# A second scan that draws dense work behind two of its three steps, with a bias moved into a gate, divided transposes and other PSUM banks

## The chip, the cores and the metric

The kernel runs on one core of a Trainium2 chip. Its time is the device time of one execution in microseconds (us); 1247.04 us is the median of three runs. The engines are PE (matrix products), DVE (element-wise work, 32x32 transposes), ACT (activations, copies), POOL, and SP, which issues DMAs. Each takes its instructions strictly in the order in which the program puts them on its queue, and waits where an operand or a buffer is not ready. PE writes into PSUM only; its banks are given out here by four tags, "mm", "aux", "e" and "us", with two tiles of 128x512 each.

## The reference, cut to what matters

The model has two residual layers, each with a token mixer and a gated FFN with a causal convolution. The mixer of the second is RWKV-7: projections, a state that is updated token by token, a norm per head, a bonus and a gate.

```python
def wkv7_scan(r, w, k, v, a, b):
    def step(state, inp):
        r_t, w_t, k_t, v_t, a_t, b_t = inp
        sa = jnp.einsum('bhvk,bhk->bhv', state, a_t)
        state = (state * w_t[:, :, None, :]
                 + sa[..., None] * b_t[:, :, None, :]
                 + v_t[..., None] * k_t[:, :, None, :])
        y_t = jnp.einsum('bhvk,bhk->bhv', state, r_t)
        return state, y_t
...
    y = wkv7_scan(r_h, decay, k_h, v_h, -kk, kk * a_h)
    mean = jnp.mean(y, -1, keepdims=True)
    var = jnp.mean(jnp.square(y - mean), -1, keepdims=True)
    y = ((y - mean) * lax.rsqrt(var + GN_EPS)).reshape(B, S, D)
    y = y * ln_w.astype(f32) + ln_b.astype(f32)
    bonus = jnp.sum(r_h * k_h * r_k.astype(f32), -1, keepdims=True) * v_h
    y = (y + bonus.reshape(B, S, D)).astype(h.dtype)
    return (y * g) @ w_o
```

There are 512 positions, 1024 channels, 16 heads of 64.

## The kernel before, in words

Activations lie transposed, as 8 tiles of 128 channels by 512 positions. Every dense product is made with a high and a low part of both operands, three matmuls of 128x512 (L325, L326, L327) for each 128 channels of the sum; we call these **dense work**. A dense product over 8 tiles of channels is thus 24 matmuls into one bank.

The mixer works on chunks of 64 positions, 8 chunks, and on two groups of 8 heads (4 tiles) each. For each group it first makes the operands and products of all chunks (`pairs`, L973 and L988, with DVE's masks at L977), inverts a triangular 64x64 matrix for each chunk and head (`invert`), and then scans over the chunks (`scan`).

*Inversion.* DVE transposes 32x32 blocks (`turn`, L1051: ix to li), eliminates column by column in pairs of operations (L1069, L1070), and transposes the result twice (ix<-li, the block inverses, and li<-li, the same once more turned). PE joins the blocks: L1090 needs ix, L1093 what came of L1090 and the second transposes, and copies on ACT lie between (L1098, L1103, L1105). Group 0 turned its 32 column blocks with one instruction, group 1 with four of 8. The inversion of group 0 ends before the first scan, that of group 1 runs beside the first scan.

*Value and bonus.* For each tile m, `projections` makes a dense product, copies it to `v` (L854), and `value` transposes it with a centring matrix (L868) and copies it out. When the pair's products are there, L883 sums the bonus per head, L885 multiplies it by v into `rt`, and L886 adds `ln_b` on ACT. The result waits in `rt` for the norm (L1366) and for the gate (L1209).

*Scan.* One chunk has five batches of small matmuls in three steps. Step 1: L1301 (us), from which `wt` is copied (L1304), and L1305. Step 2: the solve L1314, from which `vu` is copied, one half by DVE (L1315) and one by ACT (L1316). Step 3: L1321, from which the next chunk's `vu` is summed (L1325, two instructions), and L1326, from which `y` is copied (L1329). Behind each second chunk `finish` norms two chunks' y (L1342 square, L1347, L1357), transposes it (L1363) and adds it into `rt` (L1366).

*The order.* `weave` (L1467) runs the scan as `main` and draws dense work from `fill`, a chain of generators: value projections, gate products (L1135, the gates themselves L1201 to L1214), then the output product. At each `yield` of the scan a debt grows by `rate`; for each whole unit one step of `fill` (two tiles of channels, 6 matmuls, or a piece of a gate) is emitted, to be placed behind the PE instruction that ended the step `lag` steps earlier. For the second scan the rate is 0.72 and the lag 2. When the gates wait for the norm of group 0, a step of `fill` is two matmuls without use (`idle`, L1124). What the scans have not drawn comes behind them. A scheduler then settles each queue's order.

Of the kernel before, what the change touches and what calls it, by code (L numbers as in the profile page):

```python
# [12 lines left out]
F32 = mybir.dt.float32  # L13
# [7 lines left out]
P = 128  # L21
D = 1024
KT = 8
# [121 lines left out]
class Emit:  # L145
# [622 lines left out]
    def rwkv_main(self, r, ctx, gain):  # L768
# [39 lines left out]
        def projections():  # L808
# [29 lines left out]
            for m in range(KT):  # L838
                a = self.acc("mm")
                w = load.take()  # L840
                if m == KT - 2:
                    ga["w"] = load_gate(0)
                for n, _ in enumerate(self.dense_steps(a, w, xv)):
                    yield
                    next(late, None)
                    if m == KT - 1 and n == 0:
                        gw[0] = gate_weights(ga["w"])
                        ga["parts"] = self.gate_parts()
                    if m == KT - 1 and len(gx) < 2:
                        gx.append(gate_mix(len(gx)))  # L850
                for _ in late:
                    yield
                v = ip.tile([P, T], F32, tag="v", bufs=1, name=self.uid("v"))
                S.copy(v, a)  # L854
                late = value(m, v)
# [3 lines left out]
        def value(m, v):  # L859
# [21 lines left out]
            S.activation(wb, self.c("bones", P), AF.Copy, scale=self.p("r_k", m))  # L881
            q = bank()
            nc.tensor.matmul(q, wb, rt[g][:, i, :], start=True, stop=True)  # L883
            b = rt[g][:, i, :]
            V.tensor_tensor(b, q, v, ALU.mult)  # L885
            S.activation(b, b, AF.Identity, bias=self.p("ln_b", m))  # L886
            vdone.add(m)
# [139 lines left out]
        def invert(g):  # L1027
# [21 lines left out]
            def turn(out, src):  # L1049
                for bs in [slice(n, n + 8) for n in range(0, 32, 8)] if g == 1 else [slice(0, 32)]:  # L1050
                    V.transpose(out[:, bs], src[:, bs])  # L1051
# [151 lines left out]
        def gate(g, i, ts, q=None):  # L1203

            if q is None:
                q = self.acc("aux")[:, 0:ts.stop - ts.start]
                opening(g, i, ts, q)
            o = rt[g][:, i, ts]
            V.tensor_tensor(o, o, q, ALU.mult)  # L1209
            while len(outs[g]) <= i:  # L1210
                outs[g].append(tuple(self.xr.tile([P, T], F32R, tag=t, bufs=10, name=self.uid(t)) for t in ("mxh", "mxl")))
            oh, ol = (x[:, ts] for x in outs[g][i])
            S.copy(oh, o)
            V.tensor_tensor(ol, o, oh.bitcast(F32), ALU.subtract)  # L1214
# [52 lines left out]
        def scan(g, late=iter(())):  # L1267

            ih = [(i, hd) for i in range(4) for hd in (1, 0)]
            y = None  # L1270

# [11 lines left out]
            for c in range(NCH):  # L1283
# [19 lines left out]
                wt = tile_([P, 4, C], "wt", 4)  # L1303
                V.tensor_copy(wt, us[:, 0])  # L1304
                batch(lambda i, hd, n: nc.tensor.matmul(e[H[hd], 0, i, :], st[i][H[hd], 0:C], vu[H[hd], hd, i, :],  # L1305
# [5 lines left out]
                self.step(late)  # L1311
                yield
                for i, hd in ih:
# [3 lines left out]
                self.step(late)  # L1317
                yield
                lead = None
# [10 lines left out]
                self.step(late)  # L1330
                yield
                if c % 2 == 1:
# [134 lines left out]
    def weave(self, main, side, fill, rate, lag, side_rate=0.5, ktiles=2):  # L1467
# [5 lines left out]
        n0 = len(nc.cur_bb.bb.instructions)  # L1473
        for _ in main:
            new = nc.cur_bb.bb.instructions[n0:]
            pe = [i for i in new if i.engine == mybir.EngineType.PE]
            marks.extend(pe[-1:] or marks[-1:])
            due += rate
            side_due += side_rate if side else 0
# [3 lines left out]
            while due >= 1:  # L1483
                due -= 1
                if len(marks) > lag:
                    with tc.issue_after(marks[-1 - lag]):
                        next(fill, None)
# [37 lines left out]
```

## Time and profile before

| | us |
|---|---|
| median of three runs | 1247.04 |
| the runs | 1244.97, 1247.04, 1248.28 |
| profiled execution | 1245.55 |
| its span, first to last instruction | 1243.7 |
| start of the first scan's L1301, of the second scan's | 725.8, 784.2 |
| start of the second scan's last L1326 | 839.6 |
| mean granted PE clock over the span | 0.996 |

Times in the rows are in us from the span's start, durations in us or, with "mean ns", in ns. A row of the order of time has the start, the duration, the engine, the line, the operation, what it writes and reads, and in brackets how long the engine had been idle and what ended that. Matmuls are pipelined: 128x512 shows as 0.39 although the next one starts 0.23 later, so costs of PE are read from start to start. A row of a stretch has its limits and length, the busy time of PE, of PE's weight loads, of DVE, ACT and POOL, the granted PE clock, the DMA engines' share and GB/s.

### The profile page before, as it was taken

The numbers are of one execution on the slowest core, as the hardware profiler recorded it, in microseconds if no ns is written. First come the engines' busy times: TensorE is split into PE (matmuls) and PEld (weight loads), VectorE is DVE, ScalarE is ACT, GpSimd is POOL, SyncE is SP. The second block draws the span as 40 slices with busy tenths as digits, with TensorE's granted clock in tenths as the row PEclk, the third lists the DMA queues.
The fourth block names the chain that finished last, engine by engine and source line by source line (L and its number), as shares of the span: only waits on it lengthen the run. The fifth ranks groups of instructions, "written<-read, shape, count | busy, mean of one in ns | idle before, by whom it ended". The sixth has DMA issues, their size and how long they took to land.

```text
span 1243.7 us, 19411 instructions
## 1 busy us (share of the span) xinstructions
PE 1226.8 (99%) x7535; PEld 1000.2 (80%) x7535; DVE 851.1 (68%) x1418; ACT 633.1 (51%) x1089; POOL 81.4 (7%) x106
## 2 busy tenths in 40 slices
PE   9999999999999999999999999999999999999997
PEld 6878888888888888877887777778888888888886
DVE  5566578888876454675899698776777777872323
ACT  6544455555554343466787667424544444543232
POOL 1100200000000001000000013222000000000000
PEclk9999999999999999999999899999999999999999
DMA  7232457887556776326888797654223223333332
GB/s 273 94 105 82 132 180 246 246 249 241 192 172 193 220 226 196 109 81 182 220 242 237 188 280 233 219 171 135 85 102 102 90 97 102 97 88 104 97 93 81
DMA packets 125133, 201.65 MB, mean 162 GB/s; under 512 B 39857, under 2 KB 63153, under 8 KB 125041
## 3 DMA queue, kind: packets, MB, share of 16 engines
q10 hardware_dynamic: 38976, 112.87, 29.5%
q1 hardware_dynamic: 86064, 87.54, 22.6%
q8 instruction: 59, 0.97, 0.3%
q14 instruction: 34, 0.27, 0.1%
HBM read 152.93 MB, written 47.45 MB: 161 GB/s over the span
## 4 chain that ended last, share of the span: by engine, by line
PE 91%; DVE 4%; DMA 3%; ACT 1%; issue 0%; SPq 0%; POOL 0%; DVEq 0%; POOLq 0%; ACTq 0%
PE mm L325 9%; PE mm L327 9%; PE mm L326 9%; PE aux L325 6%; PE aux L326 6%; PE aux L327 6%; PE e L325 6%; PE e L326 6%; PE us L325 6%; PE e L327 6%; PE us L327 6%; PE us L326 6%; PE us L1314 1%; PE aux L973 1%; PE aux L988 1%; PE us L1321 1%
## 5 line engine op out<-in xcount | busy, mean ns | idle before, releaser
L237 ACT CAST w<-w 128x512 fp32r<-128x512 f32 x340 | 206.5, 611 | 359.8 <-PE aux L327 92.6
L238 DVE TENSOR_TENSOR w<-w,w 128x512 fp32r<-128x512 f32 x340 | 230.5, 680 | 180.2 <-ACT w L237 179.6
L325 PE MATMUL mm<-mxh,w 128*128 128x512 f32 x408 | 167.9, 412 | 2.7 <-DVE rt L885 2.6
L327 PE MATMUL mm<-mxh,w 128*128 128x512 f32 x408 | 161.1, 395 | 0.0
L326 PE MATMUL mm<-mxl,w 128*128 128x512 f32 x408 | 160.6, 394 | 0.0
L325 PEld LDWEIGHTS mm<-mxh,w 128*128 128x128 f32 x408 | 77.0, 189 | 22.8 <-DVE rt L885 3.3
L327 PEld LDWEIGHTS mm<-mxh,w 128*128 128x128 f32 x408 | 77.0, 189 | 17.1 <-issue 0.8
L326 PEld LDWEIGHTS mm<-mxl,w 128*128 128x128 f32 x408 | 77.1, 189 | 16.2 <-issue 1.7
L575 ACT ACTIVATE cv<-z,par 128x512 f32<-128x512 f32 x88 | 71.7, 817 | 26.5 <-DVE z L573 21.2
L325 PE MATMUL aux<-mxh,w 128*128 128x512 f32 x216 | 84.5, 391 | 0.0
L325 PE MATMUL us<-mxh,w 128*128 128x512 f32 x216 | 84.5, 391 | 0.0
L327 PE MATMUL aux<-mxh,w 128*128 128x512 f32 x216 | 84.2, 390 | 0.0
L326 PE MATMUL aux<-mxl,w 128*128 128x512 f32 x216 | 84.1, 389 | 0.0
L326 PE MATMUL us<-mxl,w 128*128 128x512 f32 x216 | 84.1, 389 | 0.0
L327 PE MATMUL us<-mxh,w 128*128 128x512 f32 x216 | 84.1, 389 | 0.0
L354 POOL TENSOR_TENSOR ss<-ss,sq 128x512 f32<-128x512 f32 x24 | 31.7, 1323 | 761.1 <-ACT sq L352 761.1
L325 PE MATMUL e<-mxh,w 128*128 128x512 f32 x208 | 81.4, 391 | 0.0
L326 PE MATMUL e<-mxl,w 128*128 128x512 f32 x208 | 81.1, 390 | 0.0
L327 PE MATMUL e<-mxh,w 128*128 128x512 f32 x208 | 81.0, 389 | 0.0
L576 DVE SCALAR_TENSOR_TENSOR cv<-z,par,cv 128x512 f32<-128x512 f32 x88 | 66.0, 752 | 19.5 <-ACT cv L575 19.5
L577 DVE SCALAR_TENSOR_TENSOR cv<-z,par,cv 128x512 f32<-128x512 f32 x88 | 66.0, 752 | 2.9
L325 PEld LDWEIGHTS aux<-mxh,w 128*128 128x128 f32 x216 | 40.5, 188 | 9.0 <-issue 0.5
(1113 smaller groups left out, 2555.2 us busy)
## 6 DMA issues: line engine op xcount, KB each, us to landing
w<-in_wup ACTq DMA_DIRECT2D x88, 512.0 KB, 3.7
w<-in_wdn ACTq DMA_DIRECT2D x32, 512.0 KB, 3.7
st<-std SPq DMA_DIRECT2D x15, 640.0 KB, 6.6
w<-wkd ACTq DMA_DIRECT2D x16, 512.0 KB, 5.1
w<-wvd ACTq DMA_DIRECT2D x16, 512.0 KB, 5.1
w<-wod ACTq DMA_DIRECT2D x16, 512.0 KB, 4.2
w<-in_wdn ACTq DMA_DIRECT2D x16, 384.0 KB, 3.3
w<-in_wsu ACTq DMA_DIRECT2D x8, 512.0 KB, 3.7
```

What stands on the lines that cost most here:

```text
L237: nc.scalar.copy(hi[r, :n], src)
L238: (lo_eng or nc.vector).tensor_tensor(lo[r, :n], src, hi[r, :n].bitcast(F32), ALU.subtract)
L325: mm(acc, wh, xh, start=first, stop=False)
L326: mm(acc, wh, xl, start=False, stop=False)
L327: mm(acc, wl, xh, start=False, stop=last)
L354: nc.gpsimd.tensor_tensor(self.ss, self.ss, self.sq, ALU.add)
L575: nc.scalar.activation(c, z[:, 2:], AF.Identity, scale=cw(2, i), bias=self.p("conv_b", l * 44 + i))
L576: nc.vector.scalar_tensor_tensor(c, z[:, 1:T + 1], cw(1, i), c, ALU.mult, ALU.add)
L577: nc.vector.scalar_tensor_tensor(c, z[:, 0:T], cw(0, i), c, ALU.mult, ALU.add)
L973: nc.tensor.matmul(qs[hd][:, c - ch.start, :], bk[H[hd], c, C * hd:C * hd + P], ar[H[hd], c, :], start=True, stop=True)
L988: nc.tensor.matmul(qs[hd][:, c, :], bk[H[hd], c, C * hd:C * hd + P], dg[H[hd], c, :], start=True, stop=True)
L1314: nc.tensor.matmul((us, ux)[hd][H[hd], 1, i, :], ti[g][H[hd], i, c, :], wt[H[hd], i, :], start=True, stop=True)
```

## The change

1. The second scan's `yield`s carry a factor: none behind step 1, 1.35 times the rate behind steps 2 and 3; and dense work drawn there is placed behind the step that just ended (a lag of 0).
2. `wt` is copied by ACT instead of DVE, in both scans.
3. `ln_b` is no longer added by ACT at L886 but by DVE with the gate's product, which becomes one operation with a scalar and two tensors.
4. The transposes of group 0's inversion too are made in four pieces.
5. The bonus L883 goes into a bank of "e" instead of "mm" from the point on where all keys are used and until all pairs are done; `v` has two buffers.

```diff
-                v = ip.tile([P, T], F32, tag="v", bufs=1, name=self.uid("v"))
+                v = ip.tile([P, T], F32, tag="v", bufs=2, name=self.uid("v"))
...
-            q = bank()
+            q = self.acc("aux" if len(done) == KT else "e" if KT - 1 in used else "mm")
             nc.tensor.matmul(q, wb, rt[g][:, i, :], start=True, stop=True)
             b = rt[g][:, i, :]
             V.tensor_tensor(b, q, v, ALU.mult)
-            S.activation(b, b, AF.Identity, bias=self.p("ln_b", m))
...
             def turn(out, src):
-                for bs in [slice(n, n + 8) for n in range(0, 32, 8)] if g == 1 else [slice(0, 32)]:
+                for bs in [slice(n, n + 8) for n in range(0, 32, 8)]:
                     V.transpose(out[:, bs], src[:, bs])
...
-            V.tensor_tensor(o, o, q, ALU.mult)
+            V.scalar_tensor_tensor(o, o, self.p("ln_b", 4 * g + i), q, ALU.add, ALU.mult)
...
         def scan(g, late=iter(())):
             ih = [(i, hd) for i in range(4) for hd in (1, 0)]
+            share = (0, 1.35) if g == 1 else (None, None)
...
-                V.tensor_copy(wt, us[:, 0])
+                S.copy(wt, us[:, 0])
...
                 self.step(late)
-                yield
+                yield share[0]
...
                 self.step(late)
-                yield
+                yield share[1]
...
                 self.step(late)
-                yield
+                yield share[1]
...
-        for _ in main:
+        for share in main:
             new = nc.cur_bb.bb.instructions[n0:]
             pe = [i for i in new if i.engine == mybir.EngineType.PE]
             marks.extend(pe[-1:] or marks[-1:])
-            due += rate
+            due += rate * (share or 1) if share != 0 else 0
...
             while due >= 1:
                 due -= 1
-                if len(marks) > lag:
-                    with tc.issue_after(marks[-1 - lag]):
+                back = 0 if share else lag
+                if len(marks) > back:
+                    with tc.issue_after(marks[-1 - back]):
                         next(fill, None)
```

Three places show what this does to the queues. From L887 to L1267 of the old file a line's number is one lower in the new one; in the scan the numbers agree.

**PE, group 0's inversion.** Before, from the end of the dense product into mm_6193 on; the bonus L883 has gone into mm_6277 some rows ahead:

```order
L325 MATMUL mm_6193<-mxh_5713,w_1005_6083 128x512
L326 MATMUL mm_6193<-mxl_5714,w_1005_6083 128x512
L327 MATMUL mm_6193<-mxh_5713,w_1005_6083 128x512
L325 MATMUL mm_6293<-mxh_5508,w_1020_6194 128x512
L326 MATMUL mm_6293<-mxl_5509,w_1020_6194 128x512
L327 MATMUL mm_6293<-mxh_5508,w_1020_6194 128x512
L325 MATMUL mm_6293<-mxh_5515,w_1020_6194 128x512
L326 MATMUL mm_6293<-mxl_5516,w_1020_6194 128x512
L327 MATMUL mm_6293<-mxh_5515,w_1020_6194 128x512
L868 MATMUL mm_6325<-cst,v_6291 128x128
L1090 MATMUL e_6306<-ix_6288,ti_4841 32x32 x16
L868 MATMUL mm_6325<-cst,v_6291 128x128 x3
```

Now, with the bonus in e_6278; mm_6296 is the same dense product:

```order
L327 MATMUL mm_6194<-mxh_5713,w_1005_6085 128x512
L325 MATMUL mm_6296<-mxh_5508,w_1020_6195 128x512
L326 MATMUL mm_6296<-mxl_5509,w_1020_6195 128x512
L327 MATMUL mm_6296<-mxh_5508,w_1020_6195 128x512
L325 MATMUL mm_6296<-mxh_5515,w_1020_6195 128x512
L326 MATMUL mm_6296<-mxl_5516,w_1020_6195 128x512
L327 MATMUL mm_6296<-mxh_5515,w_1020_6195 128x512
L868 MATMUL mm_6331<-cst,v_6294 128x128
L868 MATMUL mm_6331<-cst,v_6294 128x128 x3
L325 MATMUL mm_6296<-mxh_5522,w_1020_6195 128x512
L1089 MATMUL e_6312<-ix_6288,ti_4841 32x32
```

L1090 (now L1089) stands behind the same six matmuls, all four instead of one L868, and one more dense matmul.

**DVE, the same inversion.** Before, both transposes stood behind the elimination, in one instruction each:

```order
L885 TENSOR_TENSOR rt_4333<-mm_6277,v_6191 128x512
L1069 TENSOR_TENSOR pr_5815<-li_5820 128x58
L1070 TENSOR_TENSOR li_5820<-li_5820,pr_5815 128x29x2
L1064 SCALAR_TENSOR_TENSOR li_5820<-li_5820 128x30
L1051 STREAM_TRANSPOSE ix_6288<-li_5820 128x32x32
L1051 STREAM_TRANSPOSE li_6289<-li_5820 128x32x32
```

Now two pieces of li_6289 stand in the middle of the elimination,

```order
L885 TENSOR_TENSOR rt_4333<-mm_6139,v_6080 128x512
L1068 TENSOR_TENSOR pr_5815<-li_5820 128x240
L1050 STREAM_TRANSPOSE li_6289<-li_5820 128x8x32
L1069 TENSOR_TENSOR li_5820<-li_5820,pr_5815 128x16x15
L1050 STREAM_TRANSPOSE li_6289<-li_5820 128x8x32
L1068 TENSOR_TENSOR pr_5815<-li_5820 128x238
```

a third further on, and at its end ix_6288 in four pieces with the last of li_6289:

```order
L1068 TENSOR_TENSOR pr_5815<-li_5820 128x58
L1069 TENSOR_TENSOR li_5820<-li_5820,pr_5815 128x29x2
L1063 SCALAR_TENSOR_TENSOR li_5820<-li_5820 128x30
L1050 STREAM_TRANSPOSE ix_6288<-li_5820 128x8x32 x4
L1050 STREAM_TRANSPOSE li_6289<-li_5820 128x8x32
```

So three pieces of li_6289 have moved ahead of ix_6288.

**PE and ACT, the second scan.** On PE, step 1 of its fifth chunk had dense work behind it:

```order
L1301 MATMUL us_7972<-vu_7871,st_7868 64x64 x8
L1305 MATMUL e_7974<-vu_7871,st_7868 64x64 x8
L327 MATMUL mm_7851<-mxh_7864,w_1222_7633 128x512
L325 MATMUL mm_7851<-mxh_7911,w_1222_7633 128x512
L326 MATMUL mm_7851<-mxl_7912,w_1222_7633 128x512
L327 MATMUL mm_7851<-mxh_7911,w_1222_7633 128x512
L325 MATMUL mm_8025<-mxh_7795,w_1251_7846 128x512
L1314 MATMUL us_7973<-wt_7983,ti_4842 64x64
```

Now the solve follows at once:

```order
L1200 MATMUL aux_7945<-sg_6635,gw_6907 128x512
L1301 MATMUL us_7958<-vu_7850,st_7847 64x64 x8
L1305 MATMUL e_7960<-vu_7850,st_7847 64x64 x8
L1314 MATMUL us_7959<-wt_7969,ti_4842 64x64
L1314 MATMUL us_7958<-wt_7969,ti_4842 64x64
```

On ACT, at the first chunk of the second scan, where wt_7598 and vu_7516 are its copies:

```order
L1329 COPY y_7355<-e_7524 64x4x64 x2
L1304 COPY wt_7598<-us_7587 128x256
L1342 ACTIVATE ysq_7611<-y_7355 128x512
L1159 ACTIVATE sq_7664<-sq_7664 32x512
L1316 COPY vu_7516<-us_7588 64x256
L256 CAST sg_6635<-sq_7664 32x512
```

The new copy wt stands behind the copies of y, and two instructions stand between it and vu. Over the whole second scan PE's order had 21 separate runs of dense work between batches, and now has 12; with the gates its dense matmuls there are 101 instead of 113. In the first scan the runs are 19 instead of 21, and the dense matmuls 73 as before.

## The prediction

> **What bounds the kernel now.** I read the page first, then the busy time by stretches of the part that the change touches, then the order of time around its largest hole.
>
> ```profile
> PE 1226.8 (99%) x7535; PEld 1000.2 (80%) x7535; DVE 851.1 (68%) x1418; ACT 633.1 (51%) x1089; POOL 81.4 (7%) x106
> ```
>
> PE is busy for 1226.8 of 1243.7 us, so all idle time of PE in the whole kernel is 17 us. Nothing that saves work on DVE, ACT or a DMA counts unless PE waits for it. PE's own time can shrink in two further ways that the busy share hides: a lower clock, and time lost between instructions. So I cut the touched part into its stages: the first inversion (656.5 to 701.5), what follows it, the first scan, the second scan, and what follows that.
>
> ```profile
> core 0: us, PE busy (x) PEld busy (x) DVE busy (x) ACT busy (x) POOL busy (x), PEclk, DMA share, GB/s
> 656.50:701.50 45.00, 40.96 (x364) 33.01 (x364) 43.89 (x100) 25.99 (x55) 0.72 (x3) 0.96 0.87 235
> 701.50:725.80 24.30, 24.30 (x355) 19.22 (x353) 13.61 (x34) 19.70 (x34) 1.27 (x2) 0.93 0.65 175
> 725.80:784.20 58.40, 56.27 (x996) 42.73 (x997) 51.77 (x119) 39.56 (x78) 15.93 (x20) 1.00 0.83 261
> 784.20:840.20 56.00, 55.50 (x770) 42.42 (x766) 39.50 (x87) 19.81 (x44) 15.19 (x16) 1.00 0.57 186
> 840.20:852.00 11.80, 11.74 (x60) 9.35 (x59) 7.99 (x27) 3.36 (x11) 1.84 (x5) 1.00 0.40 133
> ```
>
> PE idles 4.0 us in the first stretch, not at all in the second, 2.1 us in the first scan, 0.5 us in the second and 0.06 us behind it. DVE is full in the first stretch (43.89 of 45.00) and half empty in the next. The clock is below 1 in the first two stretches only. The large hole lies here:
>
> ```profile
> 694.31 0.40 PE L327 MATMUL mm<-mxh,w 128*128 128x512 f32 x1
> 696.25 0.68 DVE L885 TENSOR_TENSOR rt<-mm,v 128x512 f32<-128x512 f32 x1
> 696.99 0.50 PE L325 MATMUL mm<-mxh,w 128*128 128x512 f32 x1 [2.28 <-DVE rt L885]
> 697.67 1.99 DVE L1051 STREAM_TRANSPOSE ix<-li 128x1024 f32<-128x1024 f32 x1
> 699.51 1.97 DVE L1051 STREAM_TRANSPOSE li<-li 128x1024 f32<-128x1024 f32 x1
> 699.72 1.01 PE L1090 MATMUL e<-ix,ti 32*32 32x32 f32 x30 [0.19 <-DVE ix L1051]
> ```
>
> A dense matmul waits 2.28 us because its "mm" bank is still held by the bonus (L883), which L885 reads late on a full DVE. Right behind, PE waits again, for the transposes of the inversion. The clock answers:
>
> ```profile
> 694.63:698.05 3.42, 1.14 (x6) 0.86 (x6) 3.14 (x11) 1.84 (x4) 0.00 (x0) 0.99 0.90 235
> 698.05:701.46 3.41, 3.22 (x40) 2.67 (x39) 3.41 (x2) 0.84 (x2) 0.00 (x0) 0.50 0.47 154
> 701.46:704.87 3.41, 3.41 (x12) 2.83 (x11) 0.02 (x1) 3.28 (x6) 0.00 (x0) 0.51 0.00 0
> ```
>
> After a stretch of 3.42 us with PE busy for 1.14, the granted clock is half for 6.8 us. Of that, 5.15 us lie behind L1090's start (699.72 to 704.87); PE has no idle time there, so they cost 2.6 us.
>
> **The change, part by part.** All sums are made against the profiled execution, 1245.55 us (span 1243.7 and 1.85 around it); the median of the runs shown is 1247.04, 1.5 above it, and I add the difference to the median.
>
> *First inversion: bank "e", second v, transposes in pieces.* With the bonus of the two later tiles in "e" and with two v buffers, the matmul at 696.99 no longer waits for L885 and can run from 694.54 (694.31 and a pitch of 0.23). But the next thing in PE's order is L1090, and L1090 waits for the last piece of the transposes ix<-li, which end a chain on DVE. That chain has no gap from 656.5 on, so whatever is put ahead of its end is added to it. Three of the four pieces of li<-li now stand ahead of it. What a piece costs is seen in the second inversion, which had pieces already:
>
> ```profile
> 715.96 2.24 DVE L1051 STREAM_TRANSPOSE li<-ix 128x256 f32<-128x256 f32 x4
> 723.30 0.35 DVE L1070 TENSOR_TENSOR li<-li,pr 128x184 f32<-128x184 f32 x1
> 723.57 0.70 DVE L1051 STREAM_TRANSPOSE li<-li 128x256 f32<-128x256 f32 x1
> 724.16 0.32 DVE L1069 TENSOR_TENSOR pr<-li 128x198 f32<-128x198 f32 x1
> ```
>
> Between L1070, which ends at 723.65, and L1069 at 724.16 one piece takes 0.5 us of DVE; four in a row take 2.24 instead of 1.99. So ix<-li ends later by 3 x 0.5 for the pieces ahead of it, 0.25 for its own division and 0.25 for that of the first transposes: 2.0, at about 701.6 and L1090 with it. PE gets there by itself near 697.2: the hole is not closed, it is moved behind the freed matmuls and becomes 4.4 us in one piece. Behind L1090 less is left: the order has one dense matmul (0.23) and three L868 fewer on that side.
>
> ```profile
> 675.36 1.05 PE L868 MATMUL mm<-cst,v 128*128 128x128 f32 x8
> 676.17 0.48 PE L325 MATMUL mm<-mxh,w 128*128 128x512 f32 x1
> ```
>
> Four L868 (8 records) take 0.81 from start to start, three 0.6. So the stage after ends 2.0 - 0.8 = **1.2 us later**. Bounds: at best the pieces cost nothing on DVE, -0.8; at worst each costs its full 0.70, +1.9. From 701.5 to 725.8 PE has no idle time, so what is late at L1090 is late at the scan's start.
>
> *The clock.* A hole of 4.4 us holds more idle time than the 2.28 us that halved it before, so I expect half clock again. Before, it lasted 6.8 us, 5.15 of them behind L1090. If it again ends with the first full stretch of 3.4 us, it lasts 3.4 to 6.8 us behind L1090's start, which costs 1.7 to 3.4 instead of 2.6: **0**, bounds -0.9 and +0.8. [...]
>
> *First scan.* The copy wt goes from DVE to ACT. On DVE it stood behind the second inversion:
>
> ```profile
> 728.28 0.62 PE L1314 MATMUL us<-wt,ti 64*64 64x64 f32 x14 [0.78 <-DVE wt L1304]
> ```
>
> That wait should go, and about 0.6 us of like ones later in the scan, of 2.1 us idle in all. The order shows two dense runs fewer between batches here (19 for 21), 0.6 us by the price below. That makes **-2.0 us**. Bounds: -2.7 (all idle time and 0.6), and +1.0: ACT has its own queue here, 39.56 of 58.40 us, and a copy behind one long ACT instruction per two chunks gives back 4 x 0.7. L886 leaves ACT and its addition joins the gate:
>
> ```profile
> L886 ACT ACTIVATE rt<-rt,par x8: 711/724/727, 671.1 to 761.2; 128x512 f32<-128x512 f32 x8
> L1316 ACT COPY vu<-us x15: 367/367/369, 736.1 to 837.7; 64x256 f32<-64x256 f32 x15
> ```
>
> Eight times 0.72 leave ACT, sixteen copies come; one of 256 elements takes 0.37 by L1316, so ACT's load is the same to 0.2 us. The gate's operation becomes one with a scalar and two tensors; L1366 is of that form (0.34 for 128x128), L1209 takes 0.28 there. The 0.06 lies on DVE, which is idle for 16.5 us in the second scan, and behind it under dense work (PE idle 0.06): nothing. If that cover went, sixteen gates would cost 1 us.
>
> *Second scan.* Dense work now follows only the solve and the last batch of a chunk. What a run of dense matmuls costs beyond itself:
>
> ```profile
> 832.86 0.69 PE L1321 MATMUL us<-vu,cbt 128*64 128x64 f32 x16
> 833.38 0.64 PE L1326 MATMUL e<-vu,st 128*64 128x64 f32 x16
> ...
> 835.45 0.68 PE L1305 MATMUL e<-vu,st 64*64 64x64 f32 x16
> 836.07 0.50 PE L325 MATMUL mm<-mxh,w 128*128 128x512 f32 x1
> 836.40 0.40 PE L326 MATMUL mm<-mxl,w 128*128 128x512 f32 x1
> 836.64 0.39 PE L327 MATMUL mm<-mxh,w 128*128 128x512 f32 x1
> 836.96 0.68 PE L1314 MATMUL us<-wt,ti 64*64 64x64 f32 x16
> ```
>
> A batch followed by one of its own shape takes 0.52, followed by dense work 0.62; the first dense matmul takes 0.33 and the last one ahead of a batch 0.32 instead of 0.23. That is 0.3 us per run. The order counts 21 runs in the second scan before and 12 now: 9 x 0.3 = -2.7 us. The dense matmuls left out of the scan (12 of 113) run behind it at the same price.
>
> What this cover hid comes into the open. For the copy wt:
>
> ```profile
> 784.25 0.64 PE L1301 MATMUL us<-vu,st 128*64 128x64 f32 x16
> 784.93 0.42 DVE L1304 COPY wt<-us 128x256 f32<-128x256 f32 x1 [0.30 <-PE us L1301]
> 785.23 0.63 ACT L1160 ACTIVATE sq<-sq 32x512 f32<-32x512 f32 x1
> 785.77 0.61 ACT L1342 ACTIVATE ysq<-y 128x512 f32<-128x512 f32 x1
> ...
> 787.59 0.69 PE L1321 MATMUL us<-vu,cbt 128*64 128x64 f32 x16
> 788.49 0.41 DVE L1325 TENSOR_TENSOR vu<-us,wt 64x256 f32<-64x256 f32 x1
> ```
>
> The copy starts 0.68 behind L1301's start and takes 0.42 (0.37 on ACT): ready at 1.1. The two batches of L1301 and L1305 occupy PE for 1.15. So in a steady chunk the solve need not wait, if ACT is free. In the first three chunks the order leaves other gaps bare. Chunk 0 has nothing between solve and L1321, and ACT's vu copy stands behind L1342 and L1160 (0.61 and 0.63): about 1.0. Chunk 1 has nothing behind its last batch, while the sums L1325 start 0.9 behind L1321, take 0.41 twice, and the two batches cover 1.1: 0.65. In chunk 2 the copy stands behind a square, a cast and a load's issue: 0.5. Small change for wt behind y: 0.2. That is +2.35, less the 0.5 of idle time that was there: +1.85. Net **-0.85 us**; bounds -3.2 (no wait at all) and +2.0 (the bare chunks and half a copy's delay, 0.35, in each of eight).
>
> *Sum*: +1.2 + 0 - 2.0 - 0.85 = -1.65: 1243.9 for a profiled execution, **1245.4** beside the median.
>
> **Rivals.** (1) *The hole closes*: PE arrives at L1090 late enough, or two stretches share the idle time, so that the clock stays full: -2.6 more, 1242.8. For it: the bank wait, which is certain to go, opened the hole. Against: DVE's chain, full for 45 us, and the half clock after a smaller hole. (2) *Both scans give what they can*: -2.7 in the first, -3.2 in the second, -0.8 ahead of them: -6.7, 1240.3. For it: DVE loses sixteen copies of 0.42. Against: ACT is full in parts of the first scan. (3) *Every wait comes back*: saved runs are paid as waits for wt and vu in both scans, and only +1.2 and -0.6 remain: 1247.6. (4) *Slower*: in the second scan ACT's queue holds wt and vu in every chunk behind one instruction of 0.62 each, since both now are in one queue with the casts and squares. No dense work covers L1301 to L1314 any more, so the eight chunks pay 8 x 1.24 = 9.9 instead of the 2.35 above: +5.9, 1252.9. From 0.96 us per chunk on, the whole is slower than before by 0.3%. For it: two such instructions in chunk 0's order. Against: ACT has 19.81 of 56 us to do there.
>
> **How the numbers follow.** 0.3%, 3.7 us, is about what a measurement of this kernel can tell from no change. My sum 0.43, (1) 0.14, (2) 0.14, (3) 0.17, (4) 0.12. Faster by over 0.3% (under 1243.3): most of (1) and (2) and the low end of my sum, 0.29. Slower (over 1250.8): (4) and a little, 0.14. Within: 0.57. The range runs from 1240.0, below (2), to 1250.0, which leaves out most of (4) and the ends of the rest.
>
> **What would show it.** Right: L1090 of the first inversion starts near 701.6 behind 4 us of PE idle time on DVE's L1051, and half clock follows; no wait of a dense matmul on L885 ahead of it; the first L1314 waits under 0.3; twelve dense runs in the second scan and PE idle 2 to 3 us there, in its first three chunks. Wrong: L1090 before 700; full clock throughout; L1314 waiting on wt in most chunks of the second scan.

## The result, and the profile after

| | before | after |
|---|---|---|
| median, same session | 1244.90 us (6 runs, 1244.41 to 1248.28) | 1251.60 us (6 runs, 1250.45 to 1253.16) |
| profiled execution, its span | 1245.55, 1243.7 | 1250.45, 1248.4 |
| mean granted PE clock of the timed runs | 0.9971 (88 runs of the experiments' sessions) | 0.9953 (6 runs) |

The ratio is 1.0052 (95% interval 1.0042 to 1.0062): **slower by 0.5%**, where 1245.4 was predicted and the range ended at 1250.0. The median of before is 1244.8 over these 88 runs; the 1.5 us that the prediction added for the three runs shown was those runs' scatter.

The stretches of after, cut where its own stages begin (columns as before: limits, length, busy time of PE, of PE's weight loads, of DVE, ACT and POOL, granted clock, DMA):

```profile
core 0: us, PE busy (x) PEld busy (x) DVE busy (x) ACT busy (x) POOL busy (x), PEclk, DMA share, GB/s
657.58:702.00 44.42, 39.31 (x337) 31.61 (x336) 43.52 (x109) 23.74 (x51) 0.73 (x3) 1.00 0.89 238
702.00:726.38 24.38, 24.38 (x380) 19.34 (x380) 13.97 (x35) 20.70 (x36) 1.34 (x2) 0.93 0.65 173
726.38:786.53 60.15, 56.35 (x996) 43.01 (x997) 49.43 (x113) 38.33 (x79) 17.29 (x20) 1.00 0.81 254
786.53:840.46 53.93, 51.16 (x754) 40.43 (x751) 35.89 (x78) 22.38 (x52) 15.18 (x16) 1.00 0.59 183
840.46:857.20 16.74, 14.82 (x81) 12.20 (x78) 9.77 (x28) 3.68 (x12) 1.84 (x5) 1.00 0.40 125
```

The stages are A, from DVE's first transpose of the first inversion to PE's first L1089 (L1090 before); B, to the first scan; the scans S1 and S2, the latter to the start of the last L1326's last matmul; and T, to the first cast L240 of the next stage. The same stages of before take 43.16, 26.07, 58.46, 55.77 and 12.47, with PE idle for 4.0, 0, 2.1, 0.5 and 0.06. All that follows takes 391.2 in both. So S1 is 1.7 longer though it works as long (56.35 for 56.33): its idle time is 3.8. Of this, 1.07 is a pause in the middle of a batch, for which the profile names no releaser (at 779.49 below; more on it with e17). S2 is 1.8 shorter, but 2.8 us of work (12 dense matmuls) left it for T, which is 4.3 longer. 1.0 us is not the change's: all of after begins stage A that much later, from a wait for the load of "wkd" weights at 588 us, which comes and goes from run to run (stage A starts between 656.1 and 659.3 in the profiles here). By stages the span grows by 1.0 ahead of A, 1.3 in A, -1.7 in B, 1.7 in S1, -1.8 in S2 and 4.3 in T, 4.7 in all.

Places in the order of time of after, first on PE, then on DVE: the hole ahead of L1089, the first scan with its first chunk and the pause, the second scan, and the end of T:

```profile
698.05 0.47 PE L325 MATMUL mm<-mxh,w 128*128 128x512 f32 x1
702.00 1.06 PE L1089 MATMUL e<-ix,ti 32*32 32x32 f32 x32 [3.47 <-DVE ix L1050]
...
731.93 0.69 PE L1321 MATMUL us<-rb,ss 128*64 128x64 f32 x16 [0.97 <-DVE rb L1315]
734.75 0.69 PE L1301 MATMUL us<-vu,st 128*64 128x64 f32 x16 [0.78 <-issue]
...
779.49 0.33 PE L1326 MATMUL e<-vu,st 128*64 128x64 f32 x3 [1.07 <-issue]
...
789.37 0.69 PE L1321 MATMUL us<-vu,cbt 128*64 128x64 f32 x16 [0.75 <-ACT vu L1316]
797.73 0.69 PE L1301 MATMUL us<-vu,st 128*64 128x64 f32 x16 [0.56 <-PE e L1326]
806.70 0.68 PE L1314 MATMUL us<-wt,ti 64*64 64x64 f32 x16 [0.71 <-ACT wt L1304]
...
851.14 0.39 PE L327 MATMUL mm<-mxh,w 128*128 128x512 f32 x1
853.45 0.47 PE L325 MATMUL mm<-mxh,w 128*128 128x512 f32 x1 [1.92 <-issue]
```

```profile
730.61 0.41 DVE L1068 TENSOR_TENSOR pr<-li 128x238 f32<-128x238 f32 x1
731.05 0.41 DVE L1069 TENSOR_TENSOR li<-li,pr 128x238 f32<-128x238 f32 x1
731.37 0.41 DVE L1315 COPY rb<-us 64x256 f32<-64x256 f32 x1
...
851.22 0.29 DVE L1213 TENSOR_TENSOR mxl<-rt,mxh 128x128 fp32r<-128x128 f32 x1
851.43 0.34 DVE L1208 SCALAR_TENSOR_TENSOR rt<-rt,par,us 128x128 f32<-128x128 f32 x1
852.46 0.29 DVE L1213 TENSOR_TENSOR mxl<-rt,mxh 128x128 fp32r<-128x128 f32 x1 [0.69 <-ACT mxh L1212]
852.67 1.28 DVE L1396 TENSOR_TENSOR h<-h,mm 128x512 f32<-128x512 f32 x2
```

The hole at 702 was forecast. At 731.9 the wait for wt is gone, and PE waits for the copy behind it instead, which stands behind the second inversion's elimination on DVE. At 853.45 the profile names no releaser, but DVE does: two L1396, which free "mm" banks, stand behind the last gate's whole chain, and the dense matmul starts when the first of them is done.

The granted clock around the hole:

```profile
698.59:702.00 3.41, 0.00 (x1) 0.00 (x1) 3.20 (x11) 0.00 (x0) 0.00 (x0) 1.00 0.88 263
702.00:705.41 3.41, 3.41 (x38) 2.86 (x39) 0.40 (x1) 2.90 (x6) 0.00 (x0) 0.50 0.01 2
705.41:708.83 3.42, 3.42 (x79) 2.75 (x79) 0.73 (x2) 1.70 (x3) 0.00 (x0) 1.00 0.82 186
```

One stretch at half clock here, two in before. The profiled execution of after is the fastest of its six, with 0.997; three of the others have 0.994 and took 1251.75 to 1253.16.

### The profile page after: what moved, and what is told of

Its sections match the earlier page's. It is cut to its first block, busy times and chain, and to the rows that moved or that the text cites. A ratio compares the mean times of both kernels' runs of the same rounds, so it can differ in the third digit from the quotient of the medians.

```text
span 1248.4 us, 19418 instructions
## 1 busy us (share of the span) xinstructions
PE 1223.8 (98%) x7535; PEld 999.7 (80%) x7535; DVE 847.2 (68%) x1411; ACT 631.8 (51%) x1097; POOL 83.2 (7%) x106
## 5 line engine op out<-in xcount | busy, mean ns | idle before, releaser
L238 DVE TENSOR_TENSOR w<-w,w 128x512 fp32r<-128x512 f32 x340 | 230.9, 681 | 182.5 <-ACT w L237 182.0
```

The costliest lines, as they stand in the source:

```text
L238: (lo_eng or nc.vector).tensor_tensor(lo[r, :n], src, hi[r, :n].bitcast(F32), ALU.subtract)
```

## The experiments

Each ran beside the kernel before on one chip, 5 to 12 runs; the ratio is to that. Stage lengths are those of the profiled execution, "half" the number of stretches of 3.41 us at half clock between the starts of A and the end of T.

| | median us | ratio (95%) | A | B | S1 | S2 | T | half |
|---|---|---|---|---|---|---|---|---|
| before | 1244.8 | | 43.16 | 26.07 | 58.46 | 55.77 | 12.47 | 2 |
| after | 1251.60 | 1.0052 (1.0042 to 1.0062) | 44.42 | 24.38 | 60.16 | 53.93 | 16.73 | 1 |
| e1 | 1250.62 | 1.0041 (1.0029 to 1.0053) | 44.38 | 24.38 | 60.14 | 56.19 | 13.21 | 1 |
| e2 | 1249.06 | 1.0031 (1.0019 to 1.0043) | 43.04 | 25.33 | 59.02 | 53.92 | 16.73 | 1 |
| e3 | 1254.73 | 1.0077 (1.0065 to 1.0089) | 44.38 | 25.62 | 60.04 | 57.47 | 18.30 | 5 |
| e4 | 1250.54 | 1.0031 (1.0016 to 1.0045) | 44.39 | 25.63 | 62.24 | 53.92 | 16.42 | 3 |
| e5 | 1249.50 | 1.0034 (1.0021 to 1.0048) | 44.40 | 24.43 | 61.72 | 53.93 | 14.84 | 2 |
| e6 | 1250.34 | 1.0045 (1.0031 to 1.0059) | 44.42 | 25.59 | 60.90 | 53.96 | 16.75 | 3 |
| e7 | 1249.37 | 1.0042 (1.0026 to 1.0058) | 43.70 | 23.83 | 58.47 | 55.88 | 16.73 | 1 |
| e8 | 1247.99 | 1.0019 (1.0009 to 1.0029) | 43.06 | 26.54 | 60.44 | 53.92 | 14.81 | 3 |
| e9 | 1249.21 | 1.0030 (1.0018 to 1.0042) | 43.08 | 26.91 | 59.44 | 55.88 | 12.48 | 1 |
| e10 | 1248.37 | 1.0031 (1.0020 to 1.0041) | 43.08 | 26.05 | 60.85 | 55.83 | 12.47 | 1 |
| e11 | 1251.46 | 1.0061 (1.0044 to 1.0079) | 44.44 | 25.90 | 59.12 | 53.92 | 16.76 | 0 |
| e12 | 1247.40 | 1.0027 (1.0016 to 1.0038) | 43.06 | 26.70 | 58.88 | 55.78 | 12.45 | 1 |
| e13 | 1244.56 | 0.9997 (0.9989 to 1.0006) | 43.59 | 23.94 | 58.83 | 55.82 | 12.48 | 1 |
| e14 | 1247.52 | 1.0024 (1.0015 to 1.0033) | 43.04 | 25.32 | 58.64 | 56.07 | 13.21 | 1 |
| e15 | 1249.25 | 1.0034 (1.0021 to 1.0047) | 43.04 | 23.77 | 58.52 | 56.06 | 14.01 | 0 |
| e16 | 1246.04 | 1.0011 (1.0002 to 1.0019) | 43.11 | 23.80 | 58.78 | 53.94 | 14.79 | 0 |
| e17 | 1251.09 | 1.0048 (1.0033 to 1.0062) | 44.46 | 22.89 | 63.45 | 54.51 | 16.75 | 2 |

**One thing undone in the changed kernel (e1 to e4).**

```diff
# e1
-            share = (0, 1.35) if g == 1 else (None, None)
+            share = (None, None)
# e2
-                for bs in [slice(n, n + 8) for n in range(0, 32, 8)]:
+                for bs in [slice(n, n + 8) for n in range(0, 32, 8)] if g == 1 else [slice(0, 32)]:
# e3
-                S.copy(wt, us[:, 0])
+                V.tensor_copy(wt, us[:, 0])
# e4, in load_out: the loads of the second half are issued by SP
+            q, self.wq = self.wq, (self.wq, nc.sync)[g]
...
```

> The changed kernel with one thing undone: dense work is drawn behind every step of the second scan again, as before. Theory, place by place: the second scan with the new rule took 53.5 us and put 2.7 us of dense work behind it, against 55.3 with the old one, so the rule itself lost 0.9 there; and the 2.08 us hole at 851 us (ScalarE's last cast behind a load's issue) came with the rule, 1.5 more than before. Both go: 1251.6 - 2.4 = 1249.2 us, and the first scan stays 60 us long with its waits for the vu copy and the sums. Rival (the rule gains 0.85, as predicted, and the loss is all in the first inversion and the first scan): 1252.4. Second rival (no place of its own, the loss comes with the sum of the parts): 1250 to 1251.

S2 and T together take 69.40 instead of 70.66: the rule loses 1.3 here. The median, 1.0 less, isn't told apart from after's. T is still 0.7 longer than before.

> The changed kernel with one thing undone: the first inversion's transposes are whole again, bank e and the second v stay. Theory: the pieces ahead of the chain's end delay the first L1090 by 2.3 us, so it starts at 699.7 to 700 again; how much comes back at the first scan's start hangs on the clock. With half clock for 6.8 us again, as before: 0.6 us, 1251.0. With half clock for 3.4 us only: 2.3, 1249.3. Rival (the delay of L1090 is from the bank and the second v, which put more ahead on DVE): L1090 stays near 702 and the time at 1251.6.

Stage A falls to 43.04, and S1 by 1.1 as well; 2.5 us in the median. In all eight profiles with pieces A takes 44.4 or 44.5, in the eleven without 43.0 to 43.2 and twice 43.6 or 43.7 (e13, e7): the pieces cost DVE's chain 1.3, not 2.0. The 1.1 of S1 is the pause, which this profile does not have; its waits for L1315 and the sums are as in after (0.95 and 0.76).

> The changed kernel with one thing undone: the copy wt goes back from ScalarE to VectorE. Theory: with wt on ScalarE, VectorE's order has more operations of the second inversion ahead of the vu copy L1315 and the sums L1325 (30, 5, 5, 4 elimination operations ahead of the first four, against 28, 6, 3, 5 in this version), and TensorE waits 1.1 and 0.9 us for them in the first chunk. Undone, these waits get shorter by about 1 us in all and the wait for wt (0.8) comes back: 1251.6 within 0.7. Rival (as predicted: wt on ScalarE takes waits away in the first scan): slower by 1 to 2 us, 1252.6 to 1253.6. Third view (most of the first scan's loss is wt's place): faster by 1.7, 1249.9.

None of the three views held: 3.1 us slower than after. S2 is 3.5 longer, and three more stretches at half clock appear, in S1, S2 and T. Two of them, each with the stretch ahead of it:

```profile
727.64:731.05 3.41, 1.83 (x32) 1.50 (x27) 3.27 (x10) 0.37 (x1) 0.00 (x0) 1.00 1.00 371
731.05:734.46 3.41, 3.41 (x16) 2.37 (x15) 2.69 (x7) 1.47 (x4) 0.09 (x1) 0.50 1.06 257
...
853.94:857.35 3.41, 1.49 (x7) 0.97 (x6) 2.62 (x9) 0.60 (x2) 0.20 (x4) 1.00 0.54 181
857.35:860.76 3.41, 3.41 (x9) 2.63 (x8) 0.22 (x1) 0.00 (x0) 0.00 (x0) 0.50 0.29 96
```

PE is busy in the stretch ahead for 1.83 and 1.49 of 3.41 us, and full in the one at half clock: half of 3.41, 1.7 us, lost each time. The waits alone, without these three, leave e3 no slower than after: S1 would take 58.3 and S2 55.8, 1.8 less than in after (1.1 of it is after's pause) and 1.8 more.

> The changed kernel, with the loads of the second half of the output projection's weights issued from SyncE instead of ScalarE. Nothing else moves on TensorE. Theory: the 2.08 us hole at 851.1 us is TensorE's wait for a bank, whose reader L1396 stands on VectorE behind the last L1213, which waits for ScalarE's last cast, which stands behind the issue of a load that waits for a weight buffer. With the load on another queue the cast runs at once and the hole shrinks to 0.3 or less: 1251.6 - 1.8 = 1249.8 us. Rival (the bank or the weights are late for another reason): the hole stays at 2 us and the time at 1251.6.

PE's idle time in the hole shrinks from 1.92 to 1.60 only, T by 0.3: the load's issue ahead of ScalarE's last cast is **not** what makes it. (What follows T is 0.5 shorter too; the median is 1.1 lower.)

**The additions behind the second scan, and wt by scans (e5, e6).** e5 takes away the order that a line of `project` gave the additions:

```diff
# e5
-                    with ExitStack() as behind:
-                        if left is None:
-                            behind.enter_context(tc.issue_after(self.last(mybir.EngineType.DVE)))
-                        V.tensor_tensor(self.h[m], self.h[m], a, ALU.add)
+                    V.tensor_tensor(self.h[m], self.h[m], a, ALU.add)
# e6
-                S.copy(wt, us[:, 0])
+                (S.copy if g else V.tensor_copy)(wt, us[:, 0])
```

> The changed kernel, but the additions L1396 of the output projection behind the second scan are no longer pinned behind VectorE's last operation of the gates. Theory: the new rule pushes 12 dense matmuls behind the scan; with them two banks are full while L1396, which frees them, stands behind the whole chain L1366, L1208, L1212, L1213 of the last batch. Without the pin one L1396 stands ahead of the chain, and the 2.08 us hole shrinks to that for the cast itself, 0 to 1.0: 1251.6 - 1.0 to 2.0 = 1249.6 to 1250.6, the part from the last L1326 to the next stage's first cast 15.7 to 14.7 us long instead of 16.73. Rival (the gate's chain is late by itself, whatever stands around it): 16.7 again and 1251.6.

Right: the addition (L1393 here) stands ahead of the chain, the hole is gone, T is 1.9 shorter.

```profile
850.90 0.68 DVE L1393 TENSOR_TENSOR h<-h,mm 128x512 f32<-128x512 f32 x1
851.50 0.60 DVE L1366 SCALAR_TENSOR_TENSOR rt<-aux,par,rt 128x128 f32<-128x128 f32 x2
...
842.26:857.10 14.84, 14.84 (x81) 12.32 (x78) 9.36 (x28) 3.68 (x11) 1.84 (x5) 1.00 0.44 141
```

> The changed kernel, with the copy wt back on VectorE in the first scan only. Theory (VectorE's order): the copy's new place lets the scheduler put more elimination operations ahead of the vu copy and the sums, and costs the first scan 1.7 us; with it undone the scan takes 58.4 us instead of 60.16 and the second stays at 53.9: 1249.9. Rival (the first scan is long because the pieces end VectorE's second inversion later, and wt's place is indifferent): 60.1 and 1251.6. Third view (as predicted, wt on ScalarE gains 0.8 and more in the first scan): 61 to 62, 1252.5 to 1253.5. A half-clock window that falls into the scan adds 1.7 to any of them.

S1 is 60.90 with one stretch at half clock in it, so 59.2 without: between theory and rival. It also holds 0.90 of the pause, after's 1.07; without that too it is 58.3 against 59.1, so the copy's place costs the first scan 0.8. The median isn't told apart from after's.

**Parts alone on the kernel before (e7, e9, e12, e13, e14, e15).**

> The kernel before with one part of the change: the rule for drawing dense work in the second scan. Everything ahead of the second scan is as before (first scan's start 725.8, second's 784.2). Theory: with wt on VectorE and nothing between L1305 and L1314, the solve waits more, the second scan takes 55.8 us as in the run with wt on VectorE (57.5 less one half-clock window), and the tail 16 to 16.7: 3.5 to 4.3 us more than before for both together, 1248.6 to 1249.4, and 1.7 more for each half-clock window that the longer holes call. Rival (the rule pays as predicted, fewer changes of shape): 1244.2 to 1245.

Theory right: S2 with T takes 4.4 us more than before, the median 4.3. PE waits for wt in S2 again (1.80 in one chunk):

```profile
786.31 0.69 PE L1322 MATMUL us<-vu,cbt 128*64 128x64 f32 x16 [1.31 <-ACT vu L1317]
804.56 0.68 PE L1315 MATMUL us<-wt,ti 64*64 64x64 f32 x16 [1.80 <-DVE wt L1305]
```

> The kernel before with one part of the change: bank e for the later bonuses and two buffers for v. Theory, as predicted for this part: the wait of 2.28 us on the bank goes, the matmuls behind it run ahead of the first L1090, which still starts at 699.7 on VectorE's chain; 0.8 us less work stands behind L1090, so the first scan starts 0.8 earlier if the half clock lasts as long as before: 1245.05 - 0.8 = 1244.2. The hole is now one of 2.5 to 3 us, so 3.4 to 6.8 us of half clock follow, -1.7 or 0 more. Rival (the hole gets longer, more half clock, no gain): 1245 to 1246.

Wrong: both bank edits alone cost 4.4 us in the median (and 2.7 of the profile's excess is a late start of A). e12 and e13 try one each.

> The kernel before with bank e for the later bonuses alone (v keeps one buffer). Theory: the loss of the run with both banks (4.4 us in the median, most of it not the clock) is bank e's: the second of these bonuses, L883, now stands nine dense matmuls later on TensorE and needs a bank that ScalarE's copy L1103 of the inversion frees; L885 on VectorE and L886 on ScalarE come later by it, and with them the copies L1046 that start the second inversion. Slower than before by 2 to 4 us, 1247 to 1249, with L1046 13 us behind the first L1090 instead of 12. Rival (the second v is the cause): as before, 1244.8 to 1245.5.

> The kernel before with two buffers for v alone (the bonus keeps its mm bank, and the wait of 2.28 us with it). Theory (bank e is the cause): as before, 1244.8 to 1245.8, the order of TensorE up to the first scan is the same as before. Rival (the second v is the cause): 1248 to 1249.

It is bank e (1.0027, e9 has 1.0030); the second v does nothing. On ACT, then on PE, in e12:

```profile
708.12 1.17 ACT L1103 COPY off<-e 32x512 f32<-32x512 f32 x2
709.63 0.83 ACT L1046 COPY ix<-ti 32x768 f32<-32x768 f32 x1 [0.34 <-issue]
711.77 0.72 ACT L886 ACTIVATE rt<-rt,par 128x512 f32<-128x512 f32 x1 [1.30 <-DVE rt L885]
713.12 1.67 ACT L1046 COPY ix<-ti 32x768 f32<-32x768 f32 x2
...
719.05 0.69 PE L1093 MATMUL e<-li,off 32*32 32x32 f32 x32 [0.85 <-ACT off L1103]
```

L883 starts 10.7 behind the first L1090 instead of 8.7, ACT waits 1.30 for its L885, and two of the three L1046 that feed the second inversion stand behind that wait. The first L1046 did not come late, as I had expected. Behind them ACT is full up to L1103, for which PE waits at 719.05. B takes 0.6 more in the profile, though half clock takes 0.8 less of it: PE idles 1.1 there, and not at all in before. So 1.5 of the 2.6 have a place; for the rest there is the lower clock of the timed runs (0.9961 for 0.9971, at most 1.2 us).

> The kernel before with the bias added in the gate and the two bank edits together. Theory: without L886, ScalarE no longer stands waiting for L885 while the second inversion's copies queue behind it, so the bank edit's loss ahead of the first scan goes: L1046 starts at most 12 us behind the first L1090, the stage up to the first scan takes 24.5 to 25.5 us; scans as before (58.5 to 59, 55.8), the tail 13.2 as in the run with the old draw (0.7 more than before, from the longer gate's place in VectorE's order). In all as before within 1 us: 1244.0 to 1246. Rival (the parts add up): the loss of the banks stays, 1248 to 1250.

B as expected, T as expected (0.7 more; e9, without the longer gate operation, has 12.48), but 2.8 us slower than before in the median. Its 11 runs fall apart: five at a clock of 0.994 or 0.995 took 1247.5 to 1249.3, six at 0.997 took 1245.5 to 1247.5.

> The run before this one without the pin on the additions L1396 behind the second scan. Theory: the 0.95 us hole behind the last L1363 shrinks, the tail 12.5 instead of 13.2: 0.7 us less than the run before this one, which would be the only version at or below the kernel before, 1243.3 to 1245.3. Rival: the hole waits for the cast itself, no change.

Wrong: T is 14.01, longer than e14's 13.21. What follows is 0.44 shorter, so 0.4 is lost in all, and PE still idles 0.78 there, for 0.95. Without the 12 extra dense matmuls, taking the pin away wins nothing.

**The clock by itself (e10, e11).** Matmuls without use right ahead of the first L1090, into the bank that it overwrites (e10: three on e9; e11: four on the changed kernel):

```diff
...
+                    if g == i == hf == 0:
+                        for _ in range(3):
+                            with tc.issue_after(self.last(mybir.EngineType.PE)):
+                                nc.tensor.matmul(ps, self.c("bones", P), self.cst[:, 0:T], start=True, stop=True)
...
```

> The run before this one (bank e and two v on the kernel before), with three 128x512 matmuls added behind which nothing waits: they write the bank that the first L1090 overwrites, and stand right ahead of it on TensorE. They take 2.8 us (L883, the same form, starts its two passes 0.46 apart) and lie in the hole. Theory of the clock as the traces show it: a 3.41 us stretch with TensorE busy for less than about 2 us is followed by a stretch at half clock, 1.7 us lost in each; with the hole filled no stretch is that idle, the clock stays full, and 2.6 to 3.4 us are won though the kernel does more: 1244.2 - 3 = 1241.2. Rival (half clock here has another cause, such as the transposes or the shape of L1090's matmuls): half clock stays and the time is that of the run before, 1244 to 1245, or up to 0.3 more.

> The changed kernel with four such matmuls ahead of the first L1090: 3.7 us in its hole of 4.2. Theory of the clock: no half clock behind L1090, 1.7 us less in a run where the hole had called one stretch and 3.4 where it had called two: 1251.6 - 1.7 to 3.4 = 1248.2 to 1249.9; holes later in the first scan and behind the second may still call their own. Rival: no effect, 1251.6.

The clock did as told: 1.00 in A and B of both profiles, where B has 0.94 in e9 and 0.93 in after. A border near 2 us of busy time isn't shown: the clock stayed full behind 1.62 us in e11 and was half behind 2.37 in e5 (rows at the end). The time did not follow. In e10 B is no shorter, since at full clock PE comes to L883 early and waits for the "e" bank (e11 waits 1.61 there too):

```profile
710.62 1.13 PE L883 MATMUL e<-rt,wb 128*128 128x512 f32 x2 [1.79 <-ACT off L1108]
```

**Several undone together (e8, e16), and bank e undone (e17).**

> The changed kernel with three things: whole transposes in the first inversion, wt on VectorE in the first scan only, and no pin on the additions behind the second scan. If the three losses add up as the places say (2.5 by whole transposes, 1.7 by wt in the first scan, 1.0 to 2.0 by the pin): 1251.6 - 5.2 to 6.2 = 1245.4 to 1246.4, as fast as before. If two of them are one loss (the pieces and wt both by way of VectorE's second inversion): 1247 to 1248.

> The combination run (whole transposes, wt on VectorE in the first scan only, no pin on the additions) with bank e undone as well: what is left of the change is the draw rule, wt on ScalarE in the second scan, the bias in the gate and the second v. Theory: bank e is what the combination still lost (2.9 us in the median, half of it by half-clock windows behind the one long hole), so this one comes to the kernel before: the second scan and the tail together 68.7 instead of 68.2, all else as before, 1244.8 to 1246. Rival (the rest of the change loses 2 us or more by itself): 1247 to 1248.

> The changed kernel with bank e alone undone. Theory: the hole ahead of the first L1089 is cut in two again by the wait for the mm bank, and L883 comes earlier. On the kernel before bank e cost 2.7 us; in the changed kernel L886 is gone from ScalarE, so it costs less, 1 to 2.5: 1249.1 to 1250.6. Rival (in the changed kernel bank e pays, as predicted, 0.8): 1252.4.

e8 is 3.6 us below after, e16 5.6, and e16 is 0.1% above before (1.0002 to 1.0019): pieces, wt in the first scan, the pinned additions and bank e make most of the loss together, 5.3 of 6.7 us. Bank e's part of that isn't shown, as the intervals of e8 and e16 overlap. The stages of e16 show what is left:

```profile
699.43:723.23 23.80, 23.80 (x386) 19.01 (x386) 15.37 (x35) 20.70 (x36) 1.38 (x2) 1.00 0.68 189
723.23:782.01 58.78, 56.34 (x997) 42.84 (x997) 51.96 (x121) 35.68 (x71) 15.11 (x20) 1.00 0.84 258
782.01:835.95 53.94, 51.17 (x754) 40.42 (x751) 35.89 (x78) 22.38 (x52) 15.19 (x16) 1.00 0.60 183
835.95:850.75 14.80, 14.80 (x82) 12.29 (x78) 9.36 (x28) 3.68 (x12) 1.84 (x5) 1.00 0.43 141
```

S2 and T are 68.74 for before's 68.24: even with its worst waits away, the draw rule wins nothing. e17 missed: bank e alone undone brings 0.5, within the scatter. B falls to 22.89, but S1 grows to 63.45, with a pause of 1.57 in the middle of a batch and two stretches at half clock behind it:

```profile
777.10 0.34 PE L1326 MATMUL e<-vu,st 128*64 128x64 f32 x4 [1.57 <-issue]
```

After has the same pause (1.07 idle at 779.49). Nothing in the profile releases it, and what it is stays open. Eleven of the nineteen profiles have it, from 0.34 to 1.60, the one of before not. No single part of the change is needed for it: e13, with the second v alone, has 0.63, and e12, with bank e alone, 0.34. Each time it comes when 9665 or 9666 of PE's recorded instructions (matmuls, weight loads and its queue's own) have started, whichever matmul of the batch is next. No version here beats the kernel before; e13 equals it.

## Why the prediction was wrong, by its own steps

The sum was -1.65; the profiled execution came out at +4.9.

- **First inversion (+1.2).** Right in kind. L1089 started at 702.00, forecast 701.6, but 1.0 of that is the late start of A: the pieces cost 1.3 (A, e2), where I had 2.0. Dividing a transpose, booked at 0.25 twice, cost 0.2 in the first (2.19 for 2.02) and nothing in ix<-li (1.90 for 1.99). Stage B was to give 0.8 back and gave 1.7, the other 0.9 being one stretch at half clock less.
- **The clock (0, bounds -0.9 and +0.8).** In the profiled execution it was a gain. In the timed runs it was a loss: the mean is 0.0018 lower, of 1248 us at most 2.2. By the runs of before, where 0.001 less goes with 0.7 us more, it is 1.2; for the mean also holds a half clock behind PE's last matmul, which takes 1.5 to 3.0 us off it in the profiles and costs nothing (in before from 1240.77 on, at 0.50 with PE busy for 0.00). The step was to take the clock of one profiled execution of before, with two stretches at half clock, as that of all. Of 88 runs of before, 40 have 0.998 or 0.999 (median 1244.1; the other 48: 1245.5). In the five profiles with the hole cut in two by six dense matmuls, as in before, four stretches at half clock follow it in all, 0 to 2 each; in the twelve with bank e and nothing put into the hole, fifteen, 0 to 2 each. So a single run can show any of these, and the long hole had half clock behind it more often (1.25 stretches a profile for 0.8), with those behind the new holes in S1, S2 and T on top.
- **First scan (-2.0, bounds -2.7 and +1.0): the largest miss, +1.7.** The wait for wt went, as forecast, but it was smaller than booked: 0.98 in before (0.78 and 0.20), not 1.4. What was late next was on DVE: the copy L1315 stands behind the elimination (a wait of 0.97), and the sums L1325 and the low part L238 cost 0.25 and 0.3 more than before. I had counted the removed waits and not walked on to the next one (rival 3's thought, priced there at zero for the first scan). So the copy's move loses 0.8 here (e6, without pauses and half clock). Another 1.07 of the +1.7 is the pause, which before's profile does not show and no run here explains. The 0.6 for two dense runs fewer did not show (PE busy 56.35 for 56.33).
- **Second scan (-0.85 without the 12 matmuls moved).** Idle time was forecast at 2.35 and is 2.77, at the forecast places (0.75 at 789.37, 0.71 for wt at 806.70). The size of a dense run's price was wrong: PE's busy time fell by 4.1, of which 2.8 are the matmuls that left, so nine runs saved 1.3, or 0.15 each where I had 0.3.
- **Behind it (nothing).** Wrong by 1.5. The matmuls left out were to run at their price, under an idle time of 0.06; but more dense work behind the scan fills the "mm" banks, and the additions that empty them are pinned behind the gates' chain (e5). My first reading, the load's issue on ACT, fell with e4.
- **Edits costed at nothing.** For the second v this held within the scatter. For the gate's longer operation it did not: the cover that the prediction relied on was not enough, and S2 and T together take 0.9 more with it (69.28 in e14, 68.36 in e9). Bank e's new place in a queue was put at nothing too: alone it costs 2.6 (e12), though undone in the changed kernel it brings only 0.5, within the scatter (e17).

Rival 4, the only one that is clearly slower, named the second scan's ACT queue, and gave 1252.9; the time was near, the mechanism was not it, since PE idles 2.77 in that scan and not 9.9.

## What to carry to other kernels

When a wait goes, walk on to the next instruction that the same engine waits for, in the new order of each queue, before booking the gain; a full in-order engine such as DVE here hands the delay on (0.97 us for L1315 in after, where 0.78 for wt had been in before). A bank is more than its tag: moving a product to another tag puts it behind that tag's readers (L883 waited 1.79 us for ACT's copy of off in e10). Work pushed out of a stage needs buffers where it lands, and whatever empties them must not be ordered behind something late (the 1.92 us at 853.45 in after). And before a hole of PE is costed, look at how many runs have the clock lowered, not at one (the 88 of before show 0.993 to 0.999), and leave out what is lowered behind PE's last matmul.

## What the runs showed of the hardware

Half clock came in stretches of 3.41 us: two in a row in before (698.05 to 704.87), one in after (702.00 to 705.41). In the stretch ahead of them PE was busy for 1.14 us in before and 0.00 in after; ahead of others it was 1.49, 1.55 and 1.83 (e3) and 1.92 (e4). The busy time alone does not tell where it came, as these show, each with the stretch that follows (e11, then e5):

```profile
851.71:855.12 3.41, 1.62 (x7) 1.39 (x8) 1.59 (x4) 0.30 (x1) 0.20 (x4) 1.00 0.49 163
855.12:858.53 3.41, 3.41 (x17) 2.81 (x16) 1.20 (x2) 1.24 (x2) 0.00 (x0) 1.00 0.18 22
...
778.77:782.18 3.41, 2.37 (x80) 1.88 (x81) 2.52 (x7) 2.91 (x7) 3.11 (x2) 1.00 0.88 264
782.18:785.59 3.41, 3.41 (x37) 2.43 (x35) 1.04 (x2) 0.85 (x2) 1.44 (x2) 0.50 0.64 224
```

What else it takes is not shown. In e3 waits of 1.6 and 1.9 us in all in a stretch (3.41 less 1.83 and 1.49) had one at half clock behind them, which cost 1.7 us more. Filling the hole with matmuls without use kept the clock at 1.00 in A and B (e10, e11) and still won no time: the ratios to before are 1.0031 (e10) for e9's 1.0030, and 1.0061 (e11) for after's 1.0052.
